# Strassen's seven products for 512-channel pieces of the two feed-forward down products (one piece in the first, two in the second)

## The chip, the cores and the metric

The kernel runs on one core of a Trainium2 chip. The metric is the device time of one execution in microseconds (us). Each time below is from the hardware profiler or from a timed execution on the chip.

## What is computed

One layer of a hybrid decoder on 256 tokens of 1024 channels: a feed-forward (SwiGLU) half step, a mixer in which a state-space branch and an attention branch run side by side, and a second feed-forward half step, each with a norm ahead and behind. The part that matters here is in both feed-forward steps (D_FF is 2816):

```python
def rmsnorm(x, g):
    y = xf * lax.rsqrt(jnp.mean(xf * xf, axis=-1, keepdims=True) + EPS)
    return y.astype(x.dtype) * g
def swiglu(x, w_gate, w_up, w_down):
    return (jax.nn.silu(x @ w_gate) * (x @ w_up)) @ w_down
h = h + 0.5 * rmsnorm(swiglu(rmsnorm(h, ffn1_pre_g), ffn1_w_gate, ffn1_w_up, ffn1_w_down), ffn1_post_g)
```

The down product is the last `@ w_down`: 256 tokens x 2816 channels times 2816 x 1024.

## The kernel before

**Split precision.** Every large matrix product is made in fp32r. A factor is split into a high part (a rounding copy, mostly on ScalarE: ACT) and a low part (the difference, on VectorE: DVE), and three products are added in PSUM: high x high, low x high and high x low. A weight comes in chunks of 1 MB (128 partitions x 2048 values). `load_to` (L139) issues the load of a chunk on SyncE's queue (SP) into one of three `raw` buffers. `split_steps` (L150) makes two `whi` and two `wlo` tiles of 128x1024 from it (L168 ACT, L171 DVE), lets the `raw` buffer go and has the next chunk loaded. `take` (L182) hands a chunk to the product and first has the splitting run on to three chunks ahead (AHEAD). The split tiles, and the high and low parts of the activations, lie in one pool (`k4`) of 29 buffers of 4 KB per partition; a split waits when no buffer is free.

**The feed-forward step** (`ffn`, L562). The gate and up products run for 11 pieces of 256 hidden channels (j = 0 to 10). For each, `mm_w` (L214) makes two accumulators for gate and two for up, in three PSUM banks (`pj`) that rotate; each accumulator takes 8 matmuls 512 wide (L219) and 8 of 256 (L218, L221). ACT copies one half of an accumulator out (L222) and DVE adds the other (L223); only then is the bank free again. DVE multiplies gate and up (L599), and `split` (L194 ACT, L195 DVE) turns the piece into `gh` and `gl`, the factors of the down product.

**The down product** (`mm_n`, L456, called at L609). The 256 tokens are two blocks b of 128, the 1024 output channels two halves q of 512: four accumulators of 128x512, each a PSUM bank (`acc`, of the five `bg` banks). A weight chunk holds 256 hidden channels, which are two steps kt of 128. For each chunk there are 2 kt x 2 blocks x 3 terms x 2 halves = 24 matmuls of 128x512 (L470). The last three chunks (TAIL) are held back and run accumulator by accumulator: block 0 half 0, block 0 half 1, block 1 half 0, block 1 half 1, with 18 matmuls each. So block 0 is ready 36 matmuls before the end, and its norm begins (`ready`, `post_norm` L431): for each half ACT sums the squares (L341), DVE multiplies with the gain (L440), then the factor 1/rms is made (on POOL after the first step, on ACT after the second) and DVE updates h (L449). After the first step PE then turns h for the mixer's norm (`turned`, L355): block 0 ahead of the last 18 matmuls, block 1 (after L400) inside the mixer's first products. After the second step the h tiles are stored (L558), which ends the program.

**What sets the order.** In the gate and up stage and in the down product up to the held chunks, a scheduler puts the instructions of each engine in order when the kernel is built; in the held part PE's order is written out. Each engine works its list in order and waits on semaphores.

Of the kernel before, what the change touches and what calls it, by code (L numbers as in the profile page):

```python
# [38 lines left out]
BG_US = 3.15  # L42
GATE_US = 1.35
SSD_US = 1.55
BREAK, STOP = object(), object()


@with_exitstack
def tile_hybrid_layer(ctx: ExitStack, tc: tile.TileContext, x, ffn1_pre_g, ffn1_w_gate, ffn1_w_up,
# [25 lines left out]
    def pj(name):  # L75

        return ps.tile([P, 512], F32, tag="pj", name=name, bufs=3)
# [5 lines left out]
    def bg(shape, name):  # L83
        return ps.tile(shape, F32, tag="bg", name=name, bufs=5)


    chunks = []

    def t_chunk(w, k0, c0):
        chunks.append((w[k0:k0 + D, c0:c0 + T].rearrange("(j p) c -> p j c", p=P), [P, KD, T]))  # L90

    def s_chunk(w, k0, c0):
        chunks.append((w[k0:k0 + 512, c0:c0 + 512].rearrange("(j p) c -> p j c", p=P), [P, 4, 512]))

    def n_chunk(w, k0):
        chunks.append((w[k0:k0 + 2 * P, :].rearrange("(j p) c -> p j c", p=P), [P, 2, D]))

    w_in2 = w_in[0]
    Z0, XS0, B0, C0, DT0, Q0, KK0, V0, G0 = 0, 2048, 4096, 4608, 5120, 5152, 6176, 7200, 8224

    def ffn_chunks(wg, wu, wd):
# [6 lines left out]
        for j in range(FF // T):  # L108
            n_chunk(wd[0], j * T)

    ffn_chunks(ffn1_w_gate, ffn1_w_up, ffn1_w_down)
    for c in range(2):
        for k0 in (0, 512):
            s_chunk(w_in2, k0, V0 + c * 512)
# [17 lines left out]
            s_chunk(da_w_branch[0], k0, c * 512)  # L132
    for c in range(4):
        n_chunk(w_out[0], c * 2 * P)
    ffn_chunks(ffn2_w_gate, ffn2_w_up, ffn2_w_down)

    raws, splits = [], []
    taken = [0]
# [1 line left out]
    def load_to(n):  # L140
        while len(raws) < min(n, len(chunks)):
            i = len(raws)
            src, shape = chunks[i]
            r = sb.tile(shape, F32, tag="raw", name=f"raw{i}", bufs=RAW_BUFS)
            nj = shape[1] // 4 if i == 0 else shape[1] // 2 if i < 4 else shape[1]
            for j in range(0, shape[1], nj):
                nc.sync.dma_start(r[:, j:j + nj, :], src[:, j:j + nj, :])
            raws.append(r)

    def split_steps(ahead=True):  # L150


        i = len(splits)
        load_to(i + 1)
        r, shape = raws[i], chunks[i][1]
        nj = shape[1] // 2
        his, los = [], []
        splits.append((his, los))
        for q in range(2):
            hi = k4([P, nj, shape[2]], f"whi{i}{q}", F32R)  # L160
            lo = k4([P, nj, shape[2]], f"wlo{i}{q}", F32R)
            his.append(hi)
            los.append(lo)
            n = 1 if i == 0 else nj
            for j in range(0, nj, n):
                js = slice(j, j + n)
                copy = nc.scalar.copy if i + q + j else nc.vector.tensor_copy
                copy(hi[:, js, :], r[:, q * nj + j:q * nj + j + n, :])  # L168
                if not i + q + j:
                    yield  # L170
                nc.vector.tensor_sub(lo[:, js, :], r[:, q * nj + j:q * nj + j + n, :], hi[:, js, :].bitcast(F32))  # L171
                yield
        raws[i] = None
        if ahead:
            load_to(i + 1 + RAW_BUFS)

    def split_to(n):

        while len(splits) < min(n, len(chunks)):
            for _ in split_steps():  # L180
                pass

    def take(ahead=AHEAD):

        i = taken[0]
        taken[0] += 1
        split_to(i + ahead)
        his, los = splits[i]
        splits[i] = None
        nj = chunks[i][1][1] // 2  # L190
# [265 lines left out]
    def mm_n(acc, acts, ready, turned, begun=lambda: None):  # L456


        n = len(acts) // 2
        held = []  # L460

        def one(i, w, parts):
            wh, wl = w
            for kt in range(2):
                ah, al = acts[2 * i + kt]
                for b, qs in parts:
                    ts = slice(b * P, (b + 1) * P)
                    for x_, w_ in ((ah, wh), (al, wh), (ah, wl)):
                        for q in qs:
                            nc.tensor.matmul(acc[b][q], x_[:, ts], w_(kt)[:, halves[q]],  # L470
                                             start=i == 0 and kt == 0 and x_ is ah and w_ is wh,
                                             stop=i == n - 1 and kt == 1 and w_ is wl)
                if i == 0:
                    begun()

        for i in range(n):
            w = take()
            if i < n - TAIL:
                one(i, w, ((0, (0, 1)), (1, (0, 1))))
            else:  # L480
                held.append((i, w))
        own_order(PE)
# [9 lines left out]
        split_to(taken[0] + AHEAD)  # L492
        ready(1)

    class Norm:

# [63 lines left out]
    def ffn(post_v, tag, ready, turned, then, products):  # L560
        gu = []

        gh = k4([P, 4, T], f"gh_{tag}0", F32R)
        gl = k4([P, 4, T], f"gl_{tag}0", F32R)
        gu += [(gh[:, m, :], gl[:, m, :]) for m in range(4)]
        sgs = []

        def evict(b, i, acc, r):
            if i == 0:
                sgs.append(k2([P, 512], f"sg_{tag}b{b}"))  # L570
                act(sgs[b], acc, AF.Silu, scale=1.0 if r is None else r)
# [12 lines left out]
        products(evict, back)  # L584
        back(1)
        del sgs
        then()
        for j in range(2, FF // T):
# [10 lines left out]
            nc.vector.tensor_tensor(sg, su, sg, ALU.mult)  # L599
            split(gh[:, o:o + 2, :], gl[:, o:o + 2, :], sg)  # L600
        if ready is store:
            act_table(EXP_LN)
        pg = load_gain(post_v, f"pg_{tag}")
        acc = [[bg([P, 512], f"acc_{tag}{b}{q}") for q in range(2)] for b in range(2)]

        def done(b):
            post_norm(b, acc[b], pg, 4.0, tag, ready is store)
            ready(b)

        mm_n(acc, gu, done, turned)  # L610


    new_u("f1")
# [687 lines left out]
```

## Time and profile before

| what | value |
|---|---|
| median of 3 runs | 744.21 us (743.74 to 744.40) |
| the profiled execution's own time | 743.95 us |
| its span, first to last instruction | 742.2 us |
| PE busy (matmuls) | 734.1 us, 99% of the span |
| DVE busy | 525.2 us, 71% |
| ACT busy | 441.1 us, 59% |
| POOL busy | 38.0 us, 5% |
| moved from memory | 136.17 MB, 185 GB/s over the span |

PE is TensorE's matmuls, PEld its weight loads, which lie beside matmuls. A row of a timeline has the start in us, the duration in us, the engine, the source line, the operation, output<-inputs and the count, and in brackets the idle time of that engine just before and what ended it. A row of a group has the count, the busy time in us and the mean duration of one in ns. Matmuls are pipelined, so a single one is shown longer than the step from one to the next.

### The profile page before, as it was taken

Reading aid. Unit: us, or ns where it says so; the run is one execution under the profiler, and the core shown is the slowest. Engines: PE = TensorE matmul, PEld = TensorE weight load, DVE = VectorE, ACT = ScalarE, POOL = GpSimd, SP = SyncE. Lnnn points to the kernel's source line nnn. Section 1 sums busy time; section 2 is a strip of 40 time slices with the busy share of each in tenths; the row PEclk is TensorE's granted clock in tenths of the full one; section 3 lists DMA queues with packets and bytes.
Section 4 is the critical chain, followed back from the end, with each engine's and each line's share of the span. In section 5 each row is a group of like instructions: output and inputs, shape, how many; then the busy total and the mean of one; then the engine's idle time right before and its main releaser. Section 6 shows DMA issues by size and latency. Waiting matters only on the chain.

```text
span 742.2 us, 11061 instructions
## 1 busy us (share of the span) xinstructions
PE 734.1 (99%) x4369; PEld 641.7 (86%) x4369; DVE 525.2 (71%) x807; ACT 441.1 (59%) x742; POOL 38.0 (5%) x72
## 2 busy tenths in 40 slices
PE   8999999999999999999999999999999999999996
PEld 7888888888889999999999888888888888888885
DVE  6986567654577888787878997684775857766612
ACT  6665557553566565959957656772664655665512
POOL 2700000000300000000000000000020000000000
PEclk9999999999999999999999999999999999999998
DMA  8884666487253647666556455374470777645701
GB/s 291 232 261 150 213 227 254 170 286 226 64 169 118 192 150 225 191 186 223 170 161 217 165 178 213 118 244 182 140 243 15 227 226 227 193 172 185 273 1 57
DMA packets 94212, 137.96 MB, mean 186 GB/s; under 512 B 2684, under 2 KB 68304, under 8 KB 94160
## 3 DMA queue, kind: packets, MB, share of 16 engines
q1 hardware_dynamic: 91488, 129.51, 53.0%
q0 software_dynamic: 2368, 7.22, 3.1%
q8 instruction: 34, 0.56, 0.3%
q10 hardware_dynamic: 304, 0.53, 0.2%
q14 instruction: 18, 0.15, 0.1%
HBM read 136.17 MB, written 1.08 MB: 185 GB/s over the span
## 4 chain that ended last, share of the span: by engine, by line
PE 98%; DMA 1%; issue 0%; DVE 0%; SPq 0%; DVEq 0%; ACT 0%
PE acc_f L470 16%; PE pup_f L219 9%; PE pg_f L219 9%; PE pws L234 6%; PE pgt L234 6%; PE pg_f L218 4%; PE pup_f L218 4%; PE pn_f L244 3%; PE pn_f L234 3%; PE acc_mx L470 3%; PE pn_mx L234 3%; PE pwd L234 3%; PE pz L205 2%; PE pxs L207 2%; PE pz L207 2%; PE pxs L205 2%
## 5 line engine op out<-in xcount | busy, mean ns | idle before, releaser
L171 DVE TENSOR_TENSOR wlo<-raw,whi 128x1024 fp32r<-128x1024 f32 (+1 forms) x246 | 291.0, 1212 | 56.1 <-ACT whi L168 54.8
L168 ACT CAST whi<-raw 128x1024 fp32r<-128x1024 f32 (+1 forms) x245 | 246.8, 1045 | 55.4 <-PE acc_f L470 19.6
L219 PE MATMUL pg_f<-u_f,whi 128*128 128x512 f32 x288 | 101.3, 396 | 0.0
L219 PE MATMUL pup_f<-u_f,whi 128*128 128x512 f32 x288 | 101.1, 396 | 0.0
L218 PE MATMUL pg_f<-u_f,wlo 128*128 128x256 f32 x252 | 70.6, 280 | 0.0
L218 PE MATMUL pup_f<-u_f,wlo 128*128 128x256 f32 x252 | 70.3, 279 | 0.0
L219 PEld LDWEIGHTS pg_f<-u_f,whi 128*128 128x128 f32 x288 | 52.8, 188 | 9.7
L219 PEld LDWEIGHTS pup_f<-u_f,whi 128*128 128x128 f32 x288 | 52.7, 188 | 9.8
L470 PE MATMUL acc_f<-whi,gh_f 128*128 128x512 f32 x176 | 58.2, 390 | 0.0
L470 PE MATMUL acc_f<-whi,gl_f 128*128 128x512 f32 x176 | 58.1, 389 | 0.0
L470 PE MATMUL acc_f<-wlo,gh_f 128*128 128x512 f32 x176 | 58.1, 389 | 0.0
L218 PEld LDWEIGHTS pg_f<-u_f,wlo 128*128 128x128 f32 x252 | 47.5, 189 | 1.8
L218 PEld LDWEIGHTS pup_f<-u_f,wlo 128*128 128x128 f32 x252 | 47.5, 189 | 1.6
L223 DVE TENSOR_TENSOR su_f<-pup_f,su_f 128x256 f32<-128x256 f32 x36 | 15.2, 422 | 40.4 <-ACT su_f L222 40.4
L470 PEld LDWEIGHTS acc_f<-whi,gl_f 128*128 128x128 f32 x176 | 33.0, 188 | 6.9
L470 PEld LDWEIGHTS acc_f<-wlo,gh_f 128*128 128x128 f32 x176 | 33.0, 188 | 6.8
L470 PEld LDWEIGHTS acc_f<-whi,gh_f 128*128 128x128 f32 x176 | 33.0, 188 | 6.8
L234 PE MATMUL pgt<-whi,u_mx 128*128 128x512 f32 x128 | 33.1, 393 | 0.0
L222 ACT COPY su_f<-pup_f 128x256 f32<-128x256 f32 x36 | 13.4, 372 | 31.4 <-PE pup_f L219 31.1
L204 PE MATMUL pxs<-u_mx,whi 128*128 128x256 f32 x128 | 31.7, 285 | 0.0
L205 PE MATMUL pz<-u_mx,whi 128*128 128x256 f32 x128 | 31.6, 284 | 0.0
L204 PE MATMUL pz<-u_mx,whi 128*128 128x256 f32 x128 | 31.6, 284 | 0.0
(310 smaller groups left out, 1432.7 us busy)
## 6 DMA issues: line engine op xcount, KB each, us to landing
raw<-in_w_in_dram SPq DMA_DIRECT2D x40, 1024.0 KB, 5.4
raw<-in_ffn_w_down_dram SPq DMA_DIRECT2D x22, 1024.0 KB, 5.5
raw<-in_ffn_w_gate_dram SPq DMA_DIRECT2D x20, 1024.0 KB, 5.7
raw<-in_ffn_w_up_dram SPq DMA_DIRECT2D x20, 1024.0 KB, 5.4
raw<-in_ssd_w_branch_dram SPq DMA_DIRECT2D x8, 1024.0 KB, 5.0
acb<-acd POOLq DMA_DIRECT2D x8, 512.0 KB, 5.3
raw<-in_da_w_branch_dram SPq DMA_DIRECT2D x4, 1024.0 KB, 5.1
raw<-in_w_out_dram SPq DMA_DIRECT2D x4, 1024.0 KB, 5.0
```

The lines of the kernel that those rows point to most:

```text
L168: copy(hi[:, js, :], r[:, q * nj + j:q * nj + j + n, :])
L171: nc.vector.tensor_sub(lo[:, js, :], r[:, q * nj + j:q * nj + j + n, :], hi[:, js, :].bitcast(F32))
L204: nc.tensor.matmul(acc[m], wh(j)[:, cs], ah(k0 + j), start=first and j == ks[0], stop=False)
L205: nc.tensor.matmul(acc[m], wh(j)[:, cs], al(k0 + j), start=False, stop=False)
L207: nc.tensor.matmul(acc[m], wl(j)[:, cs], ah(k0 + j), start=False, stop=last and j == ks[-1])
L218: nc.tensor.matmul(acc[:, :T], wl(j)[:, cs], ah(j), start=False, stop=False)
L219: nc.tensor.matmul(acc, wh(j)[:, cs], ahl(j), start=j == 0, stop=j == KD - 1)
L222: nc.scalar.copy(dst[:, m, :], acc[:, T:])
L223: nc.vector.tensor_tensor(dst[:, m, :], acc[:, :T], dst[:, m, :], ALU.add)
L234: nc.tensor.matmul(acc, a(k0 + j), b(j), start=first and i == 0, stop=last and i == 11)
L244: nc.tensor.matmul(accs[b], x_(k0 + j), w_(j), start=first and j == 0 and w_ is wh and x_ is acts[b][0], stop=last and j == 3 and w_ is wl)
L470: nc.tensor.matmul(acc[b][q], x_[:, ts], w_(kt)[:, halves[q]], start=i == 0 and kt == 0 and x_ is ah and w_ is wh, stop=i == n - 1 and kt ...
```

## The change

A 512-channel piece of the down product is a product of a 2x2 grid of blocks: tokens 2 x 128, hidden channels 2 x 256, output channels 2 x 512. The kernel before makes it with 8 block products (2 chunks of 24 matmuls). The change makes some pieces with Strassen's algorithm in Winograd's form, 7 block products of 6 matmuls. Such a piece is called a quad here. The first down product has one quad (hidden channels 512 to 1023), the second has two (512 to 1023 and 1024 to 1535). A quad takes two chunks of weights. The order of the pieces is given by a plan, in which p is a plain chunk and q a quad:

```diff
+DOWN = {"f1": "p q1 p p p p p ppp", "f2": "p q1 p p q2 p ppp"}
+FIRST, LAST = (1, 2, 3, 5, 7, 6, 4), (1, 6, 7, 2, 5, 3, 4)
```

For each quad, four sums of weight blocks are made by DVE from the two `raw` buffers (128x1024 each), and seven weight operands are split instead of four tiles per two chunks:

```diff
+        PLAIN = {1: 0, 2: 2, 3: 3}
+        SUMS = {5: (1, 0), 6: (3, 5), 7: (3, 1), 4: (2, 6)}
...
+                t = k4([P, 2, 512], f"wt{self.i}{p}")
+                nc.vector.tensor_sub(t, self.quarter(n, p), m)
...
+            load_to(self.i + 2)
+            hi = k4([P, 2, 512], f"wqh{self.i}{p}", F32R)
+            src = self.quarter(self.PLAIN[p], p) if p in self.PLAIN else self.sum_of(p)
+            nc.scalar.copy(hi, src)
...
+            lo = k4([P, 2, 512], f"wql{self.i}{p}", F32R)
+            last_lo[0] = nc.vector.tensor_sub(lo, src, hi.bitcast(F32)).ins
+            self.give_back()
```

A `raw` buffer of a quad is given back (and the next load issued) only when the last sum or split that reads it is done. In `take`, a quad's product counts as a quarter of a chunk in the distance ahead. For each quad, four sums of activation blocks are made in the gate and up stage, as soon as the piece's second half (j = 3, in the second step also j = 5) is there, and split:

```diff
+        nc.vector.tensor_tensor(v[:, 0], even[:, :, bs[1]], odd[:, :, bs[1]], ALU.add)
+        nc.vector.tensor_sub(v[:, 2], even[:, :, bs[0]], even[:, :, bs[1]])
+        nc.vector.tensor_sub(v[:, 1], v[:, 0], even[:, :, bs[0]])
+        nc.vector.tensor_sub(v[:, 3], odd[:, :, bs[0]], v[:, 1])
+        split(hi, lo, v[:, 0:3])
+        split(more[:, 0], more[:, 1], v[:, 3])
```

The products use all eight PSUM banks: 2, 3, 4 and 8 are the four accumulators, 5 the fifth `bg` bank, and 1, 6 and 7 the three `pj` banks:

```diff
+        bank = {p: bg([P, 512], f"acc_{tag}p{p}") for p in (2, 3, 5, 4, 8)}
+        bank.update({p: pj(f"acc_{tag}p{p}") for p in (1, 6, 7)})
+        acc = [[bank[2], bank[3]], [bank[4], bank[8]]]
...
+            for p in LAST if last else FIRST:
+                wh, wl = take()
+                for kt in range(2):
...
+                    for x_, w_ in ((ah, wh), (al, wh), (ah, wl)):
+                        mm(p, x_, w_(kt), last and kt == 1 and w_ is wl)
```

Behind the last quad the extra banks are combined into SBUF, and at the end each accumulator gets its share by one more addition, ahead of the norm, which then reads SBUF:

```diff
+            nc.scalar.copy(p1, bank[1])
+            m = add(u2, bank[6], p1)
+            add(u3, bank[7], u2)
+            add(u4, bank[5], u2)
+            add(c4, bank[5], u3)
...
         def done(b):
-            post_norm(b, acc[b], pg, 4.0, tag, ready is store)
+            for q in range(2):
+                nc.vector.tensor_tensor(rest[b][q], acc[b][q], rest[b][q], ALU.add)
+            post_norm(b, rest[b], pg, 4.0, tag, ready is store)
             ready(b)
```

The plain chunks ahead of and between the quads run as before (24 matmuls each). Nothing is changed in the mixer or in the gate and up products.

More of the change, by code (lines that the diff above doesn't have):

```diff
@@ L95, in n_chunk, with quad @@
     def n_chunk(w, k0):
-        chunks.append((w[k0:k0 + 2 * P, :].rearrange("(j p) c -> p j c", p=P), [P, 2, D]))
+        chunk(w[k0:k0 + 2 * P, :].rearrange("(j p) c -> p j c", p=P), [P, 2, D])
+    def quad(w, k0, products):
+        n = len(units)
+        for k in (k0, k0 + 2 * P):
+            n_chunk(w, k)
+        del units[n:]
+        q = Quad(len(chunks) - 2, products)
+        units.extend((q, p) for p in products)
+    down, QUADS = {}, {}
+    for tag, plan in DOWN.items():
+        QUADS[tag] = [int(c) for c in plan if c.isdigit()]
+        rest = [j for j in range(FF // T) if j // 2 not in QUADS[tag]]
+        down[tag] = []
+        for i, c in enumerate(plan.replace(" ", "")):
+            if c == "q":
+                down[tag].append(("q", int(plan.replace(" ", "")[i + 1])))
+            elif c == "p":
+                down[tag].append(("p", rest.pop(0)))
@@ L107, in ffn_chunks @@
             t_chunk(wu[0], 0, j * T)
-        for j in range(FF // T):
-            n_chunk(wd[0], j * T)
-    ffn_chunks(ffn1_w_gate, ffn1_w_up, ffn1_w_down)
+        for kind, j in down[tag]:
+            if kind == "q":
+                quad(wd[0], j * 2 * T, LAST if j == QUADS[tag][-1] else FIRST)
+            else:
+                n_chunk(wd[0], j * T)
+    ffn_chunks("f1", ffn1_w_gate, ffn1_w_up, ffn1_w_down)
     for c in range(2):
@@ L177, in split_to, with ahead_of @@
     def split_to(n):
-        while len(splits) < min(n, len(chunks)):
+        while len(splits) < min(n, len(units)):
+            of, p = units[len(splits)]
+            if p is not None:
+                splits.append(of.split(p))
+                continue
             for _ in split_steps():
                 pass
+    def ahead_of(i, n):
+        n *= 4
+        while n > 0 and i < len(units):
+            n -= 4 if units[i][1] is None else 1
+            i += 1
+        return i
     def take(ahead=AHEAD):
@@ L186, in take @@
         taken[0] += 1
-        split_to(i + ahead)
-        his, los = splits[i]
+        split_to(ahead_of(i, ahead))
+        (of, p), w = units[i], splits[i]
         splits[i] = None
-        nj = chunks[i][1][1] // 2
+        if p is not None:
+            return w
+        his, los = w
+        nj = chunks[of][1][1] // 2
         return (lambda j: his[j // nj][:, j % nj, :], lambda j: los[j // nj][:, j % nj, :])
@@ L454, in load_gain, with mm_n @@
         return pg
-    def mm_n(acc, acts, ready, turned, begun=lambda: None):
-        n = len(acts) // 2
+    def mm_n(acc, acts, ready, turned, begun=lambda: None, pairs=None, begin=True, taken_all=lambda: None):
+        pairs = pairs or range(len(acts) // 2)
+        n = len(pairs)
         held = []
@@ L587, in ffn @@
         then()
+        sums = {}
         for j in range(2, FF // T):
@@ L600, in ffn @@
             split(gh[:, o:o + 2, :], gl[:, o:o + 2, :], sg)
+            if j // 2 in QUADS[tag]:
+                if j % 2:
+                    sums[j // 2] = sums_of(j // 2, even, sg)
+                else:
+                    even = sg
         if ready is store:
             act_table(EXP_LN)
+        acc, rest, combine, pairs = mm_quads(gu, sums, tag)
         pg = load_gain(post_v, f"pg_{tag}")
[L604 removed]
         def done(b):
[L607 removed]
+            for q in range(2):
+                nc.vector.tensor_tensor(rest[b][q], acc[b][q], rest[b][q], ALU.add)
+            post_norm(b, rest[b], pg, 4.0, tag, ready is store)
             ready(b)
[L610 removed]
+        mm_n(acc, gu, done, turned, pairs=pairs, begin=False,
+             taken_all=combine)
     new_u("f1")
```

83 lines of the change are left out of this document (74 added, 9 removed).

## The prediction

> **What bounds the kernel now.** I read the page first: how busy each engine is, and the chain that ended last.
>
> ```profile
> span 742.2 us, 11061 instructions
> ...
> PE 734.1 (99%) x4369; PEld 641.7 (86%) x4369; DVE 525.2 (71%) x807; ACT 441.1 (59%) x742; POOL 38.0 (5%) x72
> ...
> PE 98%; DMA 1%; issue 0%; DVE 0%; SPq 0%; DVEq 0%; ACT 0%
> ...
> L470 PE MATMUL acc_f<-whi,gh_f 128*128 128x512 f32 x176 | 58.2, 390 | 0.0
> L470 PE MATMUL acc_f<-whi,gl_f 128*128 128x512 f32 x176 | 58.1, 389 | 0.0
> L470 PE MATMUL acc_f<-wlo,gh_f 128*128 128x512 f32 x176 | 58.1, 389 | 0.0
> ```
>
> PE is the path: 98% of the chain, and the last column says that it never stood idle ahead of a down matmul. The two down products are 3 x 176 = 528 matmuls. The 390 ns of one is a latency, so what one is worth must be read from the step between starts. In PE's timeline, first where halves alternate, then in the held part, where matmuls follow each other in one bank:
>
> ```profile
> 171.25 0.62 PE L470 MATMUL acc_f<-whi,gl_f 128*128 128x512 f32 x2
> ...
> 172.61 0.62 PE L470 MATMUL acc_f<-whi,gl_f 128*128 128x512 f32 x2
> ...
> 719.54 0.39 PE L470 MATMUL acc_f<-whi,gh_f 128*128 128x512 f32 x1
> ...
> 735.63 0.39 PE L470 MATMUL acc_f<-wlo,gh_f 128*128 128x512 f32 x1
> ```
>
> Six matmuls lie between the first two rows: 1.36 / 6 = 0.2267 us. Between the last two lie 71 steps (the held part is 72): 16.09 / 71 = 0.2266 us. So a chunk of 24 costs 5.44 us and a product of 6 costs 1.36 us, in one bank or in two. Last, the stages, and what the other engines do meanwhile (columns: the window, its length, busy us of PE, PEld, DVE, ACT, POOL, granted clock, DMA share, GB/s):
>
> ```profile
> 22.00:132.50 110.50, 110.50 (x625) 95.80 (x624) 78.30 (x110) 65.51 (x100) 11.66 (x18) 1.00 0.67 216
> 132.70:188.40 55.70, 55.70 (x247) 46.12 (x246) 33.11 (x31) 27.63 (x33) 0.88 (x2) 1.00 0.68 227
> 576.00:675.90 99.90, 99.90 (x575) 87.06 (x573) 68.73 (x91) 59.72 (x91) 0.63 (x1) 1.00 0.65 216
> 676.00:735.90 59.90, 59.90 (x265) 49.36 (x263) 26.67 (x28) 21.60 (x28) 0.00 (x0) 1.00 0.31 115
> ```
>
> These are gate and up, then down, of the first and of the second step. DVE is busy 71% and 69% of gate and up, but 59% and 45% of down. PE is full in all four.
>
> **The change part by part.** *What goes.* A quad has 7 x 6 = 42 matmuls for 48. Three quads save 18 x 0.2267 = **4.08 us** of PE. [...]
>
> *What DVE and ACT get.* The prices:
>
> ```profile
> L171 DVE TENSOR_TENSOR wlo<-raw,whi 128x1024 fp32r<-128x1024 f32 x242 | 288.5, 1221 | 56.1 <-ACT whi L168 54.8 <-PE pws L234 0.5
> ...
> L903 DVE TENSOR_TENSOR E<-E,cbm 128x768 f32<-128x768 f32 x16 | 15.3, 957 | 7.9 <-ACT E L261 7.9
> ...
> L223 DVE TENSOR_TENSOR sg_f<-pg_f,sg_f 128x256 f32<-128x256 f32 x36 | 15.1, 421 | 1.2 <-ACT sg_f L222 0.9
> ...
> L599 DVE TENSOR_TENSOR sg_f<-su_f,sg_f 128x512 f32<-128x512 f32 x18 | 12.4, 689 | 0.3
> ```
>
> A quad takes 4 sums and 7 low parts of 1.22 us, 13.4 us of DVE beside 9.52 us of PE; the two chunks that it replaces took 4 x 1.22 = 4.9 beside 10.88. ACT gets 7 high parts for 4, below DVE's load. So the quads run only on a lead. The activation sums add, per quad, 4 operations of 128x256 and low parts of 128x768 and 128x256: 4 x 0.42 + 0.96 + 0.42 = 3.1 us in one gate and up period.
>
> *Does the lead hold?* I walk the changed order of instructions (as built) with these durations. Anchors in the timelines:
>
> ```profile
> 659.79 5.57 SPq L147 DMA_DIRECT2D raw<-in_ffn_w_down_dram  x3
> ...
> 663.75 1.22 DVE L171 TENSOR_TENSOR wlo<-raw,whi 128x1024 fp32r<-128x1024 f32 x1
> ...
> 676.00 0.62 PE L470 MATMUL acc_f<-whi,gh_f 128*128 128x512 f32 x2
> ...
> 679.45 6.91 DVE L171 TENSOR_TENSOR wlo<-raw,whi 128x1024 fp32r<-128x1024 f32 x6 [0.26 <-ACT whi L168]
> ...
> 657.10:679.45 22.35, 22.35 (x125) 19.30 (x124) 14.86 (x21) 14.11 (x22) 0.63 (x1) 1.00 0.58 212
> ...
> raw<-in_ffn_w_down_dram SPq DMA_DIRECT2D x22, 1024.0 KB, 5.5
> ```
>
> Second step. The split of the first plain chunk ends at 663.75 + 1.22 = 665.0, and the quad's first load has landed at 659.8 + 5.5. Ahead of 679.2, the last `gl` of gate and up, the new order has six operations of 1.22 us where two were: 4.9 us more in a stretch where DVE stood idle 22.35 - 14.86 = 7.5 us. Then come five for the quad, to 685.2. PE starts at 676.0, runs the plain chunk to 681.4, and reaches the quad's last product at 681.4 + 6 x 1.36 = 689.6: **4.4 us to spare**. Next DVE splits two plain chunks, to 690.1. The second quad's two loads wait for `raw` buffers, the first for the first quad's last sum (682.7), the second for the first of these plain chunks (687.6), and the latter lands at 687.6 + 5.5 = 693.1. From there ten more operations end at 705.3; PE reaches that quad's last product at 676.0 + 3 x 5.44 + 9.52 + 8.16 = 710.0: **4.7 us to spare**. The last chunk lands near 713.2 and is split by 717; PE wants it at 719.5. First step, the same way: seven operations where two were, last split at 141 to 143 (the pool may hold one back until a product ends at 139.5), wanted at 132.7 + 5.44 + 8.16 = 146.3. So no wait of PE, and I cost the weights' work at nothing; without this cover it is priced in the second rival.
>
> *Waits in gate and up.* The new sums sit ahead of the additions that free the `pj` banks:
>
> ```profile
> 54.17 0.40 PE L219 MATMUL pup_f<-u_f,whi 128*128 128x512 f32 x1
> ...
> 59.03 0.42 DVE L223 TENSOR_TENSOR sg_f<-pg_f,sg_f 128x256 f32<-128x256 f32 x1
> ...
> 62.59 0.63 PE L219 MATMUL pup_f<-u_f,whi 128*128 128x512 f32 x2
> ```
>
> The up accumulator of j = 3 ends at 54.4. Behind it DVE now does the rest of that piece (0.42, 0.69, 0.69), the sums, their low parts, and two low parts of a weight (1.22 each), partly waiting for ACT's copies; I reach 61.9 for the addition that was done at 59.03 + 0.42. The bank is wanted at 62.8, by the second matmul of the last row. So 0.9 us to spare, at three such places (the second step repeats the pattern at j = 3 and 5). I take nothing; the bounds are nothing and about 1 us at each.
>
> *The end.* The addition from the accumulator is new, and ACT's squares wait for it:
>
> ```profile
> 736.06 0.60 ACT L341 ACTIVATE jp_f<-acc_f 128x512 f32<-128x512 f32 x1 [3.39 <-PE acc_f L470]
> 736.55 0.19 ACT L341 ACTIVATION_READ_ACCUMULATOR jp_f<-acc_f 128x1 f32 x1
> ...
> 736.78 0.69 DVE L440 TENSOR_TENSOR og_f<-acc_f,pg_f 128x512 f32<-128x512 f32 x1 [3.33 <-ACT jp_f L341]
> ...
> 737.38 1.41 DVE L449 SCALAR_TENSOR_TENSOR h<-og_f,rp_f,h 128x512 f32<-128x512 f32 x2
> ```
>
> Before, DVE's gain product waited for ACT (both read the same bank); now both read SBUF and lie side by side. But the chain goes through ACT anyway: addition 0.69, squares, rms factor, h. That is **+0.7 us**; were the factor's path shorter from SBUF it could be 0.4, and 0.9 if the addition and the squares hand over slowly.
>
> *Into the mixer.* The same addition delays h at the end of the first step:
>
> ```profile
> 186.46 1.41 DVE L449 SCALAR_TENSOR_TENSOR h<-og_f,rp_f,h 128x512 f32<-128x512 f32 x2 [0.45 <-POOL rp_f L347]
> ...
> 188.48 1.04 PE L355 MATMUL pu_mx<-ident,h 128*128 128x128 f32 x8
> ...
> 199.33 1.02 DVE L400 TENSOR_SCALAR un_mx<-h,r_mx 128x512 f32<-128x512 f32 x2 [1.89 <-POOL r_mx L347]
> ...
> 201.79 1.03 PE L355 MATMUL pu_mx<-ident,un_mx 128*128 128x128 f32 x8
> ```
>
> PE turns block 0 at 188.48; its second half of h was ready at 187.9 and is now at 188.6, wanted about 188.9 (after four turns). Block 1 was ready at 200.35, wanted from 201.79; I find it 0.7 to 1.1 later, the new addition standing behind a weight's low part. Both are hidden; bounds nothing to 0.5 us.
>
> **Sum:** -4.08 + 0.73 = -3.35. On this execution's own 743.95 that gives 740.6; the median of the runs is 0.26 higher, so **740.9 us**.
>
> **The rivals.** *1. Banks come free late.* If the sums take longer than I reckoned, PE waits three times, in gate and up. Against it: 0.9 us to spare; for it: the walk there has a dozen hand-overs between ACT and DVE. Half a microsecond over costs 1.5 in all: 742.4. At 1.1 over, the gain is gone.
>
> *2. The quads outrun their weights* (slower). In the steady down product before, splits go at the pace at which the pool's buffers come free:
>
> ```profile
> 160.75 1.23 DVE L171 TENSOR_TENSOR wlo<-raw,whi 128x1024 fp32r<-128x1024 f32 x1 [1.50 <-ACT whi L168]
> ...
> 163.47 1.23 DVE L171 TENSOR_TENSOR wlo<-raw,whi 128x1024 fp32r<-128x1024 f32 x1 [1.50 <-ACT whi L168]
> ```
>
> A pair each 2.72 us. At that pace seven pairs take 19.0 us against 9.52; a lead of four pairs (8 of the pool's 29 buffers, after 12 for activations, one gain and two chunks) covers 5.4 of the 9.5, so each quad costs 4.1. With the second step's two quads hit: 740.9 + 8.2 = 749.1; it decides from a second quad on, since one alone gives 745.0. Against it: a product of a quad frees its two buffers in 1.36 us, not 2.72, and the walk has 3 to 5 us to spare. [...]
>
> *3. The saving is partly eaten* (rivals 1 and 2 in small, both hand-overs late): 742.7 to 745.7, no difference.
>
> **How the numbers follow.** The forecast, 740.0 to 741.8 by the bounds of the end and the hand-over: 0.60. Below it (the end cheaper): 0.03. Rival 1 up to 742.7: 0.15. Rival 3: 0.09. Rival 2 and beyond: 0.13. Two runs of this kernel can be told apart from about 0.2%, 1.5 us. So faster by more is 0.60 + 0.03 + 0.15 = 0.78, within 0.09, slower 0.13. The range 739.8 to 743.4 leaves out rival 2, the upper half of rival 3 and the lowest cases.
>
> **What would show it.** 510 down matmuls, still 0.227 us apart, with PE 99% busy and no idle time in front of a `wqh` or `wql` product; the last `wql` of each quad done 3 to 5 us ahead of its first use; no wait of PE for DVE in gate and up behind j = 3 and 5; from the last matmul to the first h update 2.1 us instead of 1.4. I am wrong if PE waits at the quads (the lead), at the gate accumulators (the banks), or if single products of a quad step slower than 0.227 us.

## The result, and the profile after

The changed kernel takes **740.96 us** (median of 5 runs, 740.72 to 741.38) beside 743.74 us of the kernel before (5 runs on the same chip, 743.47 to 744.40): a ratio of 0.9961, 95% interval 0.9946 to 0.9975, so 2.8 us (0.4%) faster. Forecast were 740.9 us and a gain of 3.35. The time was met closer than the gain, and the difference is the lesson of this case.

The page of the changed kernel, the lines that answer to those shown of before (busy time by engine; the chain that ended last):

```profile
span 739.0 us, 11082 instructions
...
PE 730.3 (99%) x4351; PEld 638.4 (86%) x4351; DVE 566.8 (77%) x862; ACT 452.8 (61%) x759; POOL 39.0 (5%) x72
...
PE 99%; DMA 0%; DVE 0%; ACT 0%; DVEq 0%; issue 0%
```

PE has 18 matmuls fewer, is still busy 99% and still the whole chain. DVE took 42 us more work and ACT 12 us, beside it. The whole table of PE's waits (who waited <- for what: us, times, longest):

```profile
PE warm L406 <- POOL ident L392: 1.6, 1, 1.6
PE pu_f L451 <- DMA h<-in_x_dram: 0.2, 1, 0.2
```

Both stand in the first microseconds. No quad waits for a weight, no gate accumulator for a bank. By stages (gate and up, then down, of the first and of the second step; columns as in the prediction):

```profile
22.00:132.30 110.30, 110.30 (x623) 95.64 (x622) 85.62 (x119) 67.18 (x102) 10.73 (x15) 1.00 0.66 208
132.30:191.90 59.60, 59.60 (x267) 49.22 (x266) 43.31 (x52) 33.81 (x50) 2.70 (x5) 1.00 0.65 226
573.00:672.90 99.90, 99.90 (x574) 86.95 (x573) 77.84 (x107) 63.14 (x98) 0.00 (x0) 1.00 0.62 201
674.40:731.80 57.40, 57.40 (x253) 47.16 (x251) 42.95 (x47) 25.84 (x33) 0.63 (x1) 1.00 0.43 147
```

DVE went from 71% and 69% to 78% in gate and up, and in the second down product from 45% to 75%; PE stays full and the clock at 1.00.

Where the time went is read from the starts of matmuls at the borders of the stages. The table has all kernels of this study, times in us, each from one profiled execution but for the medians; the ratios are to runs of the kernel before on the same chip. "Lead-in" is the time to the first down matmul of the first step; "first down" runs from there to the first matrix product of the mixer, "gate and up" from the first matrix product of the second step to its first down matmul, "second down" from there to the start of the last matmul, "end" from there to the end of the span, and "rest" from the first down matmul of the first step to the end of the span. The lead-in differs by some 2 us from one profiled execution to the next, with waits for the first weights; "rest" is free of that, and stages that were not touched repeat to 0.1 us.

| kernel | median us | ratio to before, 95% interval | lead-in | first down | gate and up, 2nd step | second down | end | rest |
|---|---|---|---|---|---|---|---|---|
| before | 743.74 | | 132.71 | 60.78 | 124.67 | 59.63 | 6.59 | 609.51 |
| changed | 740.96 | 0.9961, 0.9946 to 0.9975 | 132.32 | 59.66 | 124.62 | 57.30 | 7.31 | 606.70 |
| one_quad | 742.23 | 0.9973, 0.9962 to 0.9983 | 133.06 | 59.66 | 124.67 | 58.51 | 7.31 | 608.01 |
| two_in_f1 | 740.40 | 0.9948, 0.9934 to 0.9961 | 134.10 | 58.46 | 124.67 | 57.31 | 7.31 | 605.59 |
| adjacent | 741.06 | 0.9957, 0.9945 to 0.9969 | 132.64 | 59.66 | 124.62 | 57.30 | 7.30 | 606.72 |
| plain_acts | 741.02 | 0.9956, 0.9942 to 0.9970 | 133.64 | 59.42 | 124.67 | 56.91 | 7.30 | 606.14 |
| k3_low | 740.59 | 0.9962, 0.9950 to 0.9975 | 134.44 | 59.47 | 124.68 | 57.01 | 7.31 | 606.26 |
| slow_sums | 741.40 | 0.9972, 0.9957 to 0.9987 | 132.62 | 59.66 | 124.67 | 57.31 | 7.31 | 606.77 |
| add_by_pe | 741.74 | 0.9967, 0.9954 to 0.9979 | 133.49 | 59.66 | 124.67 | 57.79 | 6.58 | 606.55 |
| two_in_f1_pe | 739.88 | 0.9953, 0.9939 to 0.9967 | 132.89 | 58.46 | 124.67 | 57.79 | 6.58 | 605.32 |
| padded | 739.72 | 0.9935, 0.9917 to 0.9953 | 133.83 | 58.25 | 124.66 | 56.91 | 7.30 | 604.98 |
| all_r0 | 739.51 | 0.9932, 0.9917 to 0.9948 | 132.83 | 58.06 | 124.68 | 56.91 | 7.30 | 604.88 |
| all_r32 | 739.63 | 0.9941, 0.9923 to 0.9960 | 133.12 | 58.06 | 124.62 | 56.90 | 7.30 | 604.76 |
| sums4 | 751.68 | 1.0095, 1.0080 to 1.0111 | 135.65 | 59.67 | 132.72 | 57.31 | 7.31 | 614.87 |

From before to after, the first down product is 1.12 us shorter (1.36 expected), the second 2.33 (2.72 expected), the end 0.72 longer: a gain of 2.73 in all, 2.81 in "rest". So 0.63 us of the 4.08 did not come. PE's timeline of the changed kernel shows where, in the first quad of the second step:

```profile
679.86 0.39 PE L619 MATMUL acc_f2p<-wqh,gh_f 128*128 128x512 f32 x1
...
682.59 0.64 PE L619 MATMUL acc_f2p<-wqh,s 128*128 128x512 f32 x2
...
689.55 0.61 PE L619 MATMUL acc_f2p<-whi,gh_f 128*128 128x512 f32 x2
```

The first two products, on plain activations (`gh_f`), are 12 steps in 2.73 us: 0.2275 each. The activations are here the stationary operand, the 128x128 one that a weight load (PEld, 188 to 189 ns each) puts in ahead of the matmul, and the weights the moving one. From the first product that takes a **sum** of activations as its stationary operand (`sh`, `sl` for three of the sums, `s` for the fourth), 30 steps take 6.96 us: 0.232. The quad lasts 9.69 us instead of 9.52, with no idle time. The two quads in the other order (`LAST`, sums from the second product on) last 9.74. Together 0.17 + 2 x 0.22 = **0.61 us**.

### The profile page after: what moved, and what is told of

Its sections match the earlier page's. It is cut to its first block, busy times and chain, and to the rows that moved or that the text cites. A ratio compares the mean times of both kernels' runs of the same rounds, so it can differ in the third digit from the quotient of the medians.

```text
span 739.0 us, 11082 instructions
## 1 busy us (share of the span) xinstructions
PE 730.3 (99%) x4351; PEld 638.4 (86%) x4351; DVE 566.8 (77%) x862; ACT 452.8 (61%) x759; POOL 39.0 (5%) x72
## 4 chain that ended last, share of the span: by engine, by line
PE 99%; DMA 0%; DVE 0%; ACT 0%; DVEq 0%; issue 0%
PE pup_f L315 9%; PE pg_f L315 9%; PE pws L330 6%; PE pgt L330 6%; PE acc_f1p L568 6%; PE acc_f2p L619 5%; PE pg_f L314 4%; PE pup_f L314 4%; PE pn_f L340 3%; PE pn_f L330 3%; PE acc_mx L568 3%; PE pn_mx L330 3%; PE pwd L330 3%; PE acc_f2p L568 3%; PE pz L301 2%; PE pxs L303 2%
## 5 line engine op out<-in xcount | busy, mean ns | idle before, releaser
L252 DVE TENSOR_TENSOR wlo<-raw,whi 128x1024 fp32r<-128x1024 f32 (+1 forms) x234 | 275.9, 1210 | 35.2 <-ACT whi L249 33.8
L249 ACT CAST whi<-raw 128x1024 fp32r<-128x1024 f32 (+1 forms) x233 | 234.0, 1044 | 34.2 <-DMA raw<-in_ffn_w_down_dram 11.3
L300 PE MATMUL pxs<-u_mx,whi 128*128 128x256 f32 x128 | 31.7, 285 | 0.0
L301 PE MATMUL pxs<-u_mx,whi 128*128 128x256 f32 x128 | 31.4, 283 | 0.0
L330 PEld LDWEIGHTS pgt<-whi,u_mx 128*128 128x128 f32 x128 | 23.6, 188 | 5.4 <-DVE yl L291 0.3
L1003 DVE SCALAR_TENSOR_TENSOR xs<-pxs,cols_b,xs 128x255 f32<-128x255 f32 (+2 forms) x48 | 21.9, 477 | 6.3 <-ACT xs L1000 5.9
L301 PEld LDWEIGHTS pz<-u_mx,whi 128*128 128x128 f32 x128 | 24.5, 192 | 0.2 <-issue 0.2
L301 PEld LDWEIGHTS pxs<-u_mx,whi 128*128 128x128 f32 x128 | 24.5, 192 | 0.0
L300 PEld LDWEIGHTS pz<-u_mx,whi 128*128 128x128 f32 x128 | 24.5, 192 | 0.0
```

The costliest lines, as they stand in the source:

```text
L300: nc.tensor.matmul(acc[m], wh(j)[:, cs], ah(k0 + j), start=first and j == ks[0], stop=False)
L301: nc.tensor.matmul(acc[m], wh(j)[:, cs], al(k0 + j), start=False, stop=False)
L330: nc.tensor.matmul(acc, a(k0 + j), b(j), start=first and i == 0, stop=last and i == 11)
L1003: nc.vector.scalar_tensor_tensor(dst[:, m, s:], acc[:, m, :T - s], cw(3 - s, c), dst[:, m, s:], ALU.mult, ALU.add)
```

## The experiments

**What is a quad worth, and does the cover hold?** Three plans. In the diffs only the line of the plan changes.

```diff
 one_quad
+DOWN = {"f1": "p q1 p p p p p ppp", "f2": "p q1 p p p p p ppp"}
 two_in_f1
+DOWN = {"f1": "p q1 p p q2 p ppp", "f2": "p q1 p p q2 p ppp"}
 adjacent
+DOWN = {"f1": "p q1 p p p p p ppp", "f2": "p q1 q2 p p p ppp"}
```

> The second down product keeps one quad of its two; its plan is one plain chunk, the quad, eight plain chunks. Theory A (a quad is worth its six matmuls less a slower step: in the changed kernel its 42 matmuls took 9.69 to 9.74 us, not 9.52, and nothing waits): one quad less costs 10.88 - 9.72 = 1.16 us, so 742.1 us against 741.0 of the changed kernel; the end stays 2.1 us from the last matmul to the first h update, since the additions stay. Rival B (the second quad of a product runs at the edge of its lead, and part of its gain is lost there): the difference is under 0.8 us, 741.3 to 741.8. Rival C (a quad is worth the full 1.36 us): 742.3.

> The first down product gets the plan of the second: two quads with two plain chunks between them, four quads in all. Theory A (no wait at the quads, 1.16 us net for each): 741.0 - 1.16 = 739.8 us, the first down product 1.16 us shorter, the end unchanged. Rival B (the first step has less lead than the second, or the three more activation sums at j = 5 hold up a gate bank there): a wait of PE of 1 us or more in the first step, 740.8 or later. The trace tells where the wait stands.

> The two quads of the second down product follow each other with no plain chunk between; as many matmuls as in the changed kernel. Theory A (a product gives its two buffers back in 1.38 us, so the second quad's splits run at VectorE's pace of 1.14 us each; the walk has its last split at about 697, wanted at 697.8, and the next plain chunk at 699.3, wanted at 699.3): no wait or up to 0.8 us of it, 741.0 to 741.8. Rival B (the recorded second rival: without plain chunks in between the splits go at 2.72 us a pair, so that a quad outruns them by 4.1 us): PE idle 3 to 5 us in the second quad, 744 to 746.

One quad less makes the second down product 1.21 us longer (58.51 for 57.30), one more makes the first 1.20 us shorter (58.46 for 59.66): 10.88 - 9.69 = 1.19 us for each, as theory A has it (it said 1.16); the medians moved by +1.3 and -0.6, the second with a lead-in 1.8 us longer in its trace. Theory C (1.36) is 0.16 off. No wait of PE behind the lead-in in any of the three. `adjacent` was the hard test of the recorded second rival, and its second down product takes 57.30 us as before. DVE's and PE's timeline of it, the last low part of the second quad and the first matmul of the product that uses it:

```profile
695.61 1.23 DVE L134 TENSOR_TENSOR wql<-wt,wqh 128x1024 fp32r<-128x1024 f32 x1
```

```profile
698.24 0.40 PE L619 MATMUL acc_f2p<-wqh,gh_f 128*128 128x512 f32 x1
```

Split by 696.84, wanted at 698.24: without the chunks between, 1.4 us of lead remain. Splits ran at DVE's own pace, 1.14 us from start to start, not at 2.72 us a pair. Rival 2 falls, with its price of 4.1 us a quad.

**Why do the products with a sum step slower?** First, the same order, weights and waits, but plain activations as the stationary operand (so the output is another one):

```diff
-                        ah, al = (x_[{5: 0, 6: 1, 7: 2, 3: 3}[p]][:, kt, :] for x_ in (sh, sl))
+                        ah, al = (x_[:, :P] for x_ in acts[4 * j + kt])
```

> In the quads the four products that take a sum of activations as the stationary operand take a plain block of the activations instead (the sums are still made, and the output is another one); weights, waits and order of the products stay. Theory A (the slower steps, 233 instead of 227 ns, come from the tiles of the sums): all 126 matmuls of the quads step by 226.7 ns, a quad takes 9.52 us, and the time falls by 0.6 us to 740.4. Rival B (they come from the semaphore waits that each product carries, one in six matmuls, or from the order of banks): steps as in the changed kernel, 741.0.

PE's timeline of `plain_acts`, first matmul of the first quad of the second step and the first after it:

```profile
681.03 0.39 PE L619 MATMUL acc_f2p<-wqh,gh_f 128*128 128x512 f32 x1
...
690.55 0.61 PE L619 MATMUL acc_f2p<-whi,gh_f 128*128 128x512 f32 x2
```

42 steps in 9.52 us, 0.2267 each, and the second down product 0.39 us shorter. So it is the tiles of the sums, and not the waits or the order of the banks (theory B). The median of whole runs did not show it (741.02); "rest" did (606.14 for 606.70). Next, the same sums in another place:

```diff
+    k3([P, 768], "k3_first")
     last_lo = [None]
```

> Same work; the pool that holds the 128x768 sums (hi and lo, taken by three of the four products with a sum) is laid at the low end of SBUF, at 36 to 49 KB of a partition instead of 215 to 227 KB; the pool of the other buffers moves up by 12 KB, the fourth sum stays in a third pool at 215 to 221 KB. Theory A (the stationary operand's place decides: what lies in the upper end of the partition is loaded a little later): the three products with `sh` and `sl` step by 226.7 ns, the one with the fourth sum stays at 232 to 234; activations that now lie above 196 KB may become slow in their place. Sum of steps in the quads 0.3 to 0.5 us less, 740.6. Theory B (it is what the tiles hold, or how they are written, not where they lie): 232 to 234 ns as in the changed kernel, 741.0.

PE's timeline of `k3_low`, from the product with the fourth sum through four products to the next chunk:

```profile
684.56 0.64 PE L620 MATMUL acc_f2p<-wqh,s 128*128 128x512 f32 x2
...
685.96 0.39 PE L620 MATMUL acc_f2p<-wqh,sh 128*128 128x512 f32 x1
...
691.40 0.62 PE L620 MATMUL acc_f2p<-whi,gh_f 128*128 128x512 f32 x2
```

The six with `s` take 1.40 us (0.233 each); the 24 behind them 5.44 us (0.2267). The addresses here and below are those of the allocator; the traces do not keep them. What the tiles hold (theory B) is out. But theory A's "upper end" fell as well: in this kernel the high part of that quad's plain activations lies at bytes 200096 to 204192 of a partition, about where the fourth sum lay in the changed kernel (202784 to 204832), and its products step at 0.2267. The pool of `sh` and `sl` had gone ahead of the others, which so moved up by its 12288 bytes, `s` too; but only `sh` and `sl`, the ones that became fast, had got another start modulo 512 bytes. Two strips of padding put that to the test, then everything on one residue, then everything on the residue of the slow ones:

```diff
+    def pad(tag, n):
+        if n and tag not in padded:
+            padded.add(tag)
+            sb.tile([P, n // 4], F32, tag=f"pad_{tag}", name=f"pad_{tag}", bufs=1)
...
+        pad("k3", 256)
         return sb.tile(shape, dt, tag="k3", name=name, bufs=K3_BUFS)
...
+        pad("k2", 384)
         return sb.tile(shape, dt, tag="k2", name=name, bufs=K2_BUFS)
```

(`all_r0`: 96 bytes ahead of all pools and 384 ahead of k2; `all_r32`: 128 and 384. All three have four quads.)

> Four quads as in two_in_f1, and two unused strips of SBUF, 384 and 256 bytes of a partition, ahead of the two upper pools. Nothing else changes; the tiles of the sums stay at the upper end. Counted in bytes modulo 512, weights, plain activations and the moving operands lie at 416 in all kernels; the sums lay at 32 in the changed kernel (232 to 234 ns), and in k3_low the three that moved lay at 416 (226.7 ns) while the fourth lay at 32 (232.6). Here the fourth sum's pool lies at 416 and that of the other three at 160. Theory A (the residue decides, not the place): the product with the fourth sum steps by 226.7 ns; those with the others too if 256 is the modulus (160 = 416 - 256), and by 232 if it is 512. The quads come to 9.52 us (or 9.69), 0.8 us less in four of them: 741.0 - 1.2 - 0.8 = 739.0 us. Theory B (the place decides, the upper end is slow): 232 to 234 ns for all four, 739.8.

> Four quads, and strips of 96 and 384 bytes that put every large pool (weights, activations, sums, moving operands) at residue 0 modulo 512 instead of 416. Theory A (what counts is that stationary and moving operand lie at the same residue): plain and quad products 226.7 ns, as in padded. Theory B (416 modulo 512 is by itself a good residue and others are not): plain products 232 or more, some 2 to 3 us longer in the down products. Gate and up, whose steps of 512 columns take 233 ns beside those of 256, tell whether their step too hangs on it: 118 us shorter or longer than 126.2 less 8 of the start is not expected by either.

> Four quads, as in padded and all_r0, with strips of 128 and 384 bytes that put weights, activations, sums and moving operands alike at residue 32 modulo 512: the residue at which the sums were slow in the changed kernel, now shared by all. Theory A (a stationary operand is late where its residue modulo 256 is another than that of the rest): nothing differs, all products step by 226.7 ns, down products as in padded and all_r0 (58.1 to 58.3 and 56.9 us), 739.6. Theory B (32 modulo 256 is slow by itself, 160 and 0 are not): plain products and quads alike take 232 to 234 ns, 24 matmuls 0.13 us longer, the down products 1.4 us longer each, and more in every other product of the kernel: above 744.

PE's timeline, the first quad of the second step, of `padded` and of `all_r32`:

```profile
680.05 0.39 PE L628 MATMUL acc_f2p<-wqh,gh_f 128*128 128x512 f32 x1
...
689.58 0.62 PE L628 MATMUL acc_f2p<-whi,gh_f 128*128 128x512 f32 x2
```

```profile
679.12 0.39 PE L630 MATMUL acc_f2p<-wqh,gh_f 128*128 128x512 f32 x1
...
688.64 0.39 PE L630 MATMUL acc_f2p<-whi,gh_f 128*128 128x512 f32 x1
```

9.53 and 9.52 us: all quads of both, and of `all_r0`, step by 0.2267. `padded` differs from `two_in_f1` by the two strips alone, and there the quads last 9.69 and 9.74. The starts of the tiles, from the allocator's table of each built kernel, in bytes modulo 512:

| kernel | weights (moving), plain activations | `sh`, `sl` | `s` | step with `sh`, `sl` | step with `s` |
|---|---|---|---|---|---|
| changed | 416 | 32 | 32 | 232 to 234 ns | 232 to 234 |
| k3_low | 416 | 416 | 32 | 226.5 to 228 | 233 |
| padded | 416 | 160 | 416 | 226.7 | 226.7 |
| all_r0 | 0 | 0 | 0 | 226.7 | 226.7 |
| all_r32 | 32 | 32 | 32 | 226.7 | 226.7 |

Neither the place nor the residue is slow by itself: 32 is fast where all share it, 160 beside 416 (256 apart) is fast, 32 beside 416 (384 apart) is slow. In these five kernels the step goes with the distance of the sums' start from that of the other operands, counted modulo 512: at 384 bytes a matmul takes some 6 ns more (232 to 234 for 226.7), at 0 and 256 nothing more. No other distance was run, and the modulus is the author's choice, which the runs don't fix. Whether the partner is the moving operand or the stationary operand ahead isn't told apart here. Nor does every slow step come from a distance: the 512-wide matmuls of gate and up, which alternate with 256-wide ones, step by 233 ns in the kernel before (median of 251 in the second step) and by some 230 in `all_r32`, and the stage lasts 124.67, 124.68 and 124.62 us in the kernel before, `all_r0` and `all_r32`, which is what the expectation for `all_r0` asked. `all_r0` and `padded` (and `all_r32`) are faster than both kernels: 739.5 to 739.7 us, "rest" 1.7 to 1.9 us below the changed kernel, 1.1 of it from the fourth quad (`two_in_f1`). The medians don't show the padding by itself: `padded`'s 739.72 lies nearer to theory B's 739.8 than to theory A's 739.0; the steps decide. Its first down product is 0.19 us longer than that of `all_r0` for another reason: PE takes 1.22 us for 1.04 to turn block 0 of h, whose second half is ready only at 187.39, 0.5 us after the turn began.

**The gate banks (rival 1).** The first activation sum is made twice over, and then four times.

```diff
-        nc.vector.tensor_tensor(v[:, 0], even[:, :, bs[1]], odd[:, :, bs[1]], ALU.add)
+        for _ in range(2):
+            nc.vector.tensor_tensor(v[:, 0], even[:, :, bs[1]], odd[:, :, bs[1]], ALU.add)
```

(`sums4`: `range(4)`.)

> The first of the four activation sums is made twice over (128x256, some 0.34 us more of VectorE for each quad); by the order of instructions this also puts one more low part of a weight (1.14 us) ahead of the additions that free the gate banks. The changed kernel's addition ended at 61.4 and its bank was wanted at 62.4. Theory A (rival 1 of the prediction: about 0.9 to 1.0 us to spare at each of three places, and what goes over it stands as a wait of PE): the addition comes 1.5 us later, PE waits 0.5 to 0.6 us at three places, 1.5 to 1.8 us in all, 742.5 to 742.8. Rival B (the hand-overs leave more room than the walk says): no wait, 741.0.

No wait, and this says little: the expectation misread the order. No further low part stands ahead of the addition, which came only 0.3 us later than in the changed kernel and stayed inside the spare time of both theories. Hence the stronger dose:

> The first activation sum of each quad is made four times over; by the order of instructions the addition that frees the gate banks now has three more sums (0.34 us each) and two more low parts of weights (1.14 us each) ahead of it: 3.3 us. In the changed kernel it ended at 61.44 and the bank was wanted at 62.42. Theory A (rival 1 of the prediction: 1.0 us to spare at each of three places, the rest is a wait of PE): 2.3 us at each, 6.5 to 7.3 us in all, 747.5 to 748.3. Rival B (the delay is taken up elsewhere): no wait at the gate banks, under 742.

Of `sums4`: DVE's timeline with the additions that free the banks; PE's table of waits; the windows of one wait and of what follows (PEclk is the third number from the end):

```profile
65.14 0.75 DVE L319 TENSOR_TENSOR sg_f<-pg_f,sg_f 128x256 f32<-128x256 f32 x2
```

```profile
PE pup_f L315 <- DVE sg_f L319: 6.6, 3, 2.2
```

```profile
608.00:610.00 2.00, 0.07 (x1) 0.00 (x0) 2.00 (x4) 0.83 (x4) 0.00 (x0) 1.00 1.09 383
610.00:611.00 1.00, 0.75 (x4) 0.70 (x5) 0.86 (x3) 0.44 (x1) 0.00 (x0) 0.92 1.07 317
611.00:614.00 3.00, 3.00 (x11) 2.52 (x10) 0.00 (x0) 0.19 (x1) 0.00 (x0) 0.50 0.77 256
614.00:615.00 1.00, 1.00 (x6) 0.86 (x6) 0.00 (x0) 0.08 (x1) 0.00 (x0) 0.87 0.00 0
638.50:641.50 3.00, 3.00 (x11) 2.51 (x11) 0.13 (x1) 0.37 (x1) 0.00 (x0) 0.50 0.36 117
```

PE waits at exactly three places, 2.2 us each: the 3.3 us added less the 1.0 to spare, as rival 1's mechanism has it. The time, though, rose by 10.7 us, not 6.5 to 7.3. In the second step gate and up is 8.1 us longer (132.72 for 124.62), of which the two waits are 4.4. Most of the rest is the clock: behind each of them it stands at 0.50 for 3.4 us ((0.08 + 3 x 0.5 + 0.13) / 0.5), which costs half of that, 1.7 us, twice. Behind the wait of the first step the clock stayed at 1.00.

The traces also show where the clock falls. In `sums4` it does so at 610.84 and 638.15, 27.31 us apart, which is 8 times 3.413, and a slow stretch is as long (3.4 us). Behind the last matmul it falls 730.45 us after its first rise in the kernel before (7.73 to 738.18) and 727.04 us after it in the changed kernel (7.50 to 734.54), 214 and 213 times 3.413. So these four falls fit a grid of 3.413 us; that step is an estimate from them. The windows of `sums4` on that grid, two around the wait of the first step, then two for each wait of the second:

```profile
61.30:64.70 3.40, 2.13 (x13) 1.57 (x11) 3.40 (x5) 2.06 (x5) 0.00 (x0) 1.00 0.73 233
64.72:68.12 3.40, 2.51 (x14) 2.24 (x15) 1.50 (x5) 0.63 (x1) 0.00 (x0) 1.00 1.05 351
607.44:610.84 3.40, 1.22 (x8) 0.81 (x7) 3.40 (x7) 1.51 (x5) 0.00 (x0) 1.00 1.05 352
610.85:614.25 3.40, 3.40 (x13) 2.92 (x12) 0.01 (x1) 0.34 (x1) 0.00 (x0) 0.50 0.73 239
634.74:638.14 3.40, 1.48 (x8) 1.33 (x9) 2.53 (x6) 1.08 (x3) 0.00 (x0) 1.00 1.07 360
638.15:641.56 3.41, 3.41 (x12) 2.90 (x11) 0.19 (x1) 0.37 (x1) 0.00 (x0) 0.50 0.43 141
```

The first wait is cut in two by the grid, so PE is idle for 37% and 26% of the two windows, and neither is followed by a slow one. The other two fall into one window each (64% and 56% idle), and the next window runs at half clock. The end is alike in two more traces: PE is idle for 63% of 734.77 to 738.18 in the kernel before and for 71% of 731.12 to 734.53 in the changed one, and from there the clock stands at 0.50. In `padded` 730.24 to 733.64, around its last matmul, is 51% idle, and no slow window follows: the mean clock of that run is 0.999, for 0.997 in the changed kernel, where the last 4.5 us are slow.

**The end.** The combined tile is put into the last accumulator by PE, with an identity, instead of being added by DVE behind the last matmul:

```diff
+        def last_bank():
+            for x_ in by_pe[1:]:
+                nc.tensor.matmul(acc[1][1], by_pe[0], x_, start=False, stop=False)
...
                 if q == 1 and i == n - TAIL:
                     turned()
+                    last_bank()
```

> The last of the additions at the end (the combined products onto the last accumulator, 0.69 us after the last matmul) is taken off VectorE: the combined tile is split into a high and a low part and two matmuls with an identity put it into the bank ahead of the last products. Theory A (the end's +0.7 us is this addition in the chain): from the last matmul to the first h update 1.4 us instead of 2.06, two matmuls of 0.23 us more: net -0.2 to -0.25 us, 740.7. Rival B (the squares or the gain product are late for another reason): the end stays above 1.9 us, and the time rises by 0.45 us to 741.4. The difference is below what whole runs tell apart; the trace decides.

> Both: two quads in the first down product as well, and the last addition by two matmuls. If both stand for themselves: 741.0 - 1.2 - 0.2 = 739.6 us, no wait of PE at a quad; PE's own end in the trace 1.2 us earlier less the 0.45 us of the two matmuls. If the quads of the first product cost elsewhere (into the mixer, at the gate banks): above 740.2.

In the changed kernel, PE's, DVE's and ACT's timelines of the end:

```profile
731.71 0.39 PE L568 MATMUL acc_f2p<-wlo,gh_f 128*128 128x512 f32 x1
```

```profile
732.14 0.69 DVE L779 TENSOR_TENSOR c_f<-acc_f2p,c_f 128x512 f32<-128x512 f32 x1 [2.44 <-PE acc_f2p L568]
732.86 0.69 DVE L536 TENSOR_TENSOR og_f<-c_f,pg_f 128x512 f32<-128x512 f32 x1
734.18 1.41 DVE L545 SCALAR_TENSOR_TENSOR h<-og_f,rp_f,h 128x512 f32<-128x512 f32 x2 [0.63 <-ACT rp_f L357]
```

```profile
732.86 0.63 ACT L437 ACTIVATE jp_f<-c_f 128x512 f32<-128x512 f32 x1 [3.35 <-DVE c_f L779]
```

From the end of the last matmul at 732.10 to the first h update at 734.18 are 2.08 us; before, 736.02 to 737.38, 1.36. The gain product now lies beside the squares (both start at 732.86), and still DVE waits 0.63 us for the rms factor: the addition is in the chain whole. PE's and DVE's timelines of `add_by_pe`:

```profile
733.46 0.39 PE L569 MATMUL acc_f2p<-wlo,gh_f 128*128 128x512 f32 x1
```

```profile
735.21 1.41 DVE L545 SCALAR_TENSOR_TENSOR h<-og_f,rp_f,h 128x512 f32<-128x512 f32 x2
```

735.21 - 733.85 = 1.36 us, as before the change, for two matmuls more (second down product 57.79 for 57.30): net 0.24 us in the parts, 0.15 in "rest". The medians can't show it: that of `add_by_pe` is higher (741.74, near rival B's 741.4), with a lead-in 1.2 us longer in its trace. In `two_in_f1_pe` both gains stand side by side (58.46, 57.79, 6.58): 739.88 us for 739.6 expected. It was not run together with the padding.

## Why the prediction was right, and where not

1. **"Three quads save 18 x 0.2267 = 4.08 us"**: the count is right (4369 to 4351), the step failed in its price, which it took from plain products for all 126 matmuls of the quads. They step by 0.2267 to 0.228 ahead of the first sum, by 0.232 to 0.234 with sums, and by 0.229 to 0.2325 on plain activations between and behind them: the term is 3.47 us, 0.61 short. The prediction named a slower step as a sign of error, but gave it neither price nor chance. No product steps faster: the lowest mean in the changed kernel is 0.2267 us.
2. **The lead of the weights** held as walked. Its DVE rows in the changed kernel, the last splits of the two quads of the second step:

```profile
680.93 2.51 DVE L134 TENSOR_TENSOR wql<-wt,wqh 128x1024 fp32r<-128x1024 f32 x2
...
701.92 1.23 DVE L134 TENSOR_TENSOR wql<-wt,wqh 128x1024 fp32r<-128x1024 f32 x1
```

   They end at 683.4 and 703.2; the products that use them start at 688.2 and 708.8. So 4.7 and 5.6 us to spare, for 4.4 and 4.7 by the walk. In the first step the last split ends at 140.8 (141 to 143 by the walk), and its product starts at 146.1. Rival 2 did not come about, since products of a quad free buffers twice as fast as chunks do (a pair in 1.36 to 1.40 us, for 2.72), which its own counter-argument said. Its price doesn't follow from its own figures either: with four pairs of lead, the other three at 2.72 us are done after 8.16 us, just when the seventh product starts (6 x 1.36), so its pace would cost nothing rather than 4.1 us.
3. **The gate banks**: the changed kernel's row in DVE's timeline

```profile
61.02 0.74 DVE L319 TENSOR_TENSOR sg_f<-pg_f,sg_f 128x256 f32<-128x256 f32 x2
```

   has the first addition done at 61.44, the bank was taken at 62.42: 1.0 us to spare for 0.9 walked. Costed at nothing, rightly. Rival 1's mechanism is real (`sums4`), and its price of the waits holds, but it left out the clock.
4. **The end, +0.7**: it was 0.72, by the chain that the prediction gave, and it went with the addition (`add_by_pe`).
5. **Into the mixer**: no wait of PE. Block 1 of h came some 1.7 us later against the matmuls around it, not 0.7 to 1.1: before, it was ready 1.44 us ahead of the turn (200.35 for 201.79), now 0.23 us behind its start (200.50 for 200.27). The first four of the eight turns don't need its second half, and the fifth starts at 200.70, so it was hidden with 0.2 us to spare. The changed kernel's rows, DVE's and PE's:

```profile
199.48 1.02 DVE L496 TENSOR_SCALAR un_mx<-h,r_mx 128x512 f32<-128x512 f32 x2 [1.90 <-POOL r_mx L443]
```

```profile
200.27 1.03 PE L451 MATMUL pu_mx<-ident,un_mx 128*128 128x128 f32 x8
```
6. **The sum**: -4.08 + 0.73 = -3.35 should have been -3.47 + 0.72 = -2.75, and -2.78 was measured between medians. That 740.9 was met nonetheless is luck: the median of before was 744.21 in the three runs at hand and 743.74 in the five beside the result, 0.47 us that stood against the missing 0.6.

## What to carry to other kernels

Take the step of a matmul from a stream with the same operands as the new one, and look where the allocator puts a new stationary operand: here 640 bytes of padding took back what an unlucky start cost (a quad of 9.53 us for 9.69, `padded`). Where an engine has slack, a walk in order through its list with measured durations says within 1 us whether extra work fits; where it does not fit on a PE-bound kernel, a slower clock behind the wait may come on top of it (1.7 us behind each of two waits in `sums4`). Gains below the scatter of whole runs (here 1 to 2 us in the lead-in) are read from stages, not from medians.

## What the runs showed of the hardware

- In the down products a 512-wide fp32r matmul steps by 226.7 ns (`before`, `padded`, `all_r0`, `all_r32`); by 232 to 234 in the changed kernel, where its stationary operand starts 384 bytes (modulo 512) away from the other operands. Matmuls on plain activations behind such a stretch are slow too (231 ns in the product between two with sums, 229 and 232.5 in the last product of a quad). The records of the changed kernel show only later starts, no wait and no longer weight load (188 to 189 ns in both). The cause inside PE stays open.
- In `sums4` an idle time of PE of 2.2 us was followed, at two places of three, by 3.4 us at half clock. In the windows of 3.413 us fitted above, shares of 56% to 71% idle were followed by a slow stretch (`sums4`, the kernel before, the changed kernel), shares of 26%, 37% and 51% were not (`sums4`, `padded`); no share between was seen. So the same wait cost 1.7 us more at two places and nothing more at the third.
